# Expert stream of a two-block network: the copy of gathered rows traced ahead of the second split, the split of the middle columns traced one block later

## The chip, the cores and the metric

The kernel runs on one NeuronCore of a Trainium2 chip. The metric is the device time of one execution in microseconds; the time given for a kernel is the median of its runs. Engines are named as in the profile: PE is the tensor engine, PEld its weight loads, DVE the vector engine, ACT the scalar engine, POOL GpSimd, and SP the engine that issues the loads of weights.

## What is computed

The program is two blocks of two layers each. The first block is a sparse attention mixed with a gated delta rule. Each layer of the second block has a mixer, a mixture of experts and a gated addition. The change lies in the mixture of experts, which is run twice. Of 512 tokens, each goes to 2 of 32 experts:

```python
def expert_block(args):
    idx, e = args
    xb = x_pad[idx]
    hb = jax.nn.silu(xb @ w_gate[e]) * (xb @ w_up[e])
    return hb @ w_down[e]
```

`w_gate` and `w_up` of an expert are 1024 x 512, `w_down` is 512 x 1024, all fp32: 6 MB of weights per expert. The time of the kernel is that of the whole program; the two expert stages are some 530 and 515 us of it.

## The kernel before

**Precision.** A product of fp32 operands is built from rounded parts. `split(h, l, x)` (L423) writes the rounded value `h` with an ACT copy (L425) and the rest `l = x - h` with a DVE subtraction (L426). PE then multiplies the rounded parts. For the last rows of a weight tile the product is instead done with the plain fp32 tile (`also`), and there the gathered rows are needed as one whole tile, `xf`.

**Experts in pairs.** `gather` (L1517) fetches the rows of two experts, 64 slots each, with one indirect DMA issued by POOL. After that PE transposes them in two halves into PSUM (tile `aux`, L1532), and each half is split into the tile `pk` (ACT copy L425, DVE subtraction L426). Of the second half ACT also copies the last 128 rows whole, into `xf` (L1538).

**Units.** `experts` (L1727) walks over units (e, k, part). For expert e, k = 0, 1 are the two 1 MB loads of `w_gate`, k = 2, 3 those of `w_up`, k = 4, 5 those of `w_down`; each load is used in two parts, except that of k = 5, which is one unit. The order is the eight units of gate and up of expert e, then the three of down of expert e - 1. The loop runs the splits of the weights `AHEAD` = 6 units in front of the matmuls: step n splits unit n (`cut`, ACT L425 and DVE L426, into `X` or `wh` and `wl`), then does the matmuls of unit n - 6 (`inner`, L1581 to L1584, or `outer`, L1609 to L1614). Loads go through 6 buffers `w`; SP issues a load (L1561) when the buffer's last user, PE or DVE, is done with it.

**What else stands at fixed steps.** When the sum of gate or of up is complete, ACT copies it from PSUM into `tmp` (L1765), which frees one of three `acc` buffers. In the second step of expert e, `middle` (L1586) makes the hidden columns of expert e - 1: PE folds (L1593), ACT takes the tanh (L1596), DVE multiplies twice (L1597, L1598) into `mth`, and `split` turns that into `hk` (ACT, then DVE). `hk` is used by `outer` at the end of expert e. In the step (2, 1) of every odd expert the second part of `gather` (transposes, `pk`, `xf`) for the next pair is traced. `finish` (ACT L1622, DVE L1623, POOL L1624) adds the two halves of the result and scatters it.

**Order.** `pin` (L1627) binds PE, DVE and ACT each to the order in which the steps are traced, so that an instruction which waits on one of these engines holds up everything traced behind it on this engine. Within one step the scheduler may reorder.

The matmul of a new expert's gate (L1581) takes the `acc` buffer of the up sum before it, so it waits for the second of the two `tmp` copies. In trace order ACT does that copy behind the splits of the unit six steps on.

Of the kernel before, what the change touches and what calls it, by code (L numbers as in the profile page):

```python
# [20 lines left out]
P = 128  # L21
# [14 lines left out]
BLK = 64  # L36
# [143 lines left out]
class Net:  # L180
# [1336 lines left out]
    def gather(self, table, idx, m):  # L1517

        nc = self.nc
        v, act, pe = nc.vector, nc.scalar, nc.tensor  # L1520
        xg = self.t([P, D], "xg", 2)
        nc.gpsimd.indirect_dma_start(out=xg[:m], out_offset=None, in_=table[:, :],  # L1522
                                     in_offset=bass.IndirectOffsetOnAxis(ap=idx, axis=0),
                                     bounds_check=S - 1, oob_is_err=False)
        yield
        n = m // BLK
        pk = self.t([P, KT, n, P], "pk", 2, FR)
        xf = self.t([P, n, BLK], "xf", 2)
        for half in range(2):
            tp = self.aux()  # L1530
            for k in range(4):
                pe.transpose(tp[:, k * m:(k + 1) * m], xg[:m, (4 * half + k) * P:(4 * half + k + 1) * P],  # L1532
                             self.ident[:m, :m])
            tv = tp[:, 0:4 * m].rearrange("p (k e t) -> p k e t", k=4, e=n)
            o = pk[:, 4 * half:4 * half + 4]
            self.split(o[:, :, :, 0:BLK], o[:, :, :, BLK:P], tv)
            if half:
                act.activation(xf, tv[:, 3], AF.Copy)  # L1538
        yield [(pk[:, :, e], xf[:, e]) for e in range(n)]

    def apart(self, ins, first):
# [7 lines left out]
    def weights(self, i, e, k, part=None):  # L1549

        src = self.a[("w_exp_gate_2", "w_exp_up_2", "w_exp_down_2")[k // 2]][i]
        n, first = (4, 0) if part is None else (2, 2 * part)
        w = self.t([P, n * S], *(("w", self.nw) if part is None else ("wo", 1)))
        first += k % 2 * 4
        if k < 4:
            at, ap = first * S, [[D * D_EXP // P, P], [1, n * S]]
        else:
            at, ap = first // 2 * P * D, [[D, P], [P * D, n // 2], [1, D]]  # L1560
        self.load = self.nc.sync.dma_start(w if k < 4 else w.rearrange("p (f n) -> p f n", n=D), bass.AP(  # L1561
            tensor=src.tensor, offset=src.offset + e * (D * D_EXP) + at, ap=ap))
        return w.rearrange("p (q n) -> p q n", n=S)
# [22 lines left out]
    def middle(self, gu):  # L1586

        nc = self.nc
        v, act, pe = nc.vector, nc.scalar, nc.tensor
        fp = self.aux()  # L1590
        for q in range(2):
            for f in range(4):
                pe.matmul(fp[:, (4 * q + f) * BLK:(4 * q + f + 1) * BLK], gu[q][:, f * P:(f + 1) * P], self.fold,  # L1593
                          start=True, stop=True)
        th = self.t([P, 4 * BLK], "mth", 2)
        act.activation(th, fp[:, 0:256], AF.Tanh, scale=0.5)  # L1596
        v.scalar_tensor_tensor(th, th, 1.0, fp[:, 0:256], op0=OP.add, op1=OP.mult)  # L1597
        v.scalar_tensor_tensor(th, th, 0.5, fp[:, 256:512], op0=OP.mult, op1=OP.mult)  # L1598
        hk = self.t([P, 4, P], "hk", 2, FR)
        hv = th.rearrange("p (f t) -> p f t", f=4)  # L1600
        self.split(hk[:, :, 0:BLK], hk[:, :, BLK:P], hv)
        return hk, hv

    def outer(self, pss, hid, k, h, l, also):

# [94 lines left out]
    def overflow(self, i, e, x, mp, ym):  # L1700

        room = lambda: self.t([P, S], "bc", 3)
        gu = []
        for up in range(2):
            ps = self.acc()
            for k in range(0, KT, 2):
                w = self.weights(i, e, 2 * up + k // 4, k // 2 % 2)
                m = 1 if k == KT - 2 else 2
                h, l = self.cut(w[:, 0:m])
                self.inner(ps, x, k, h[:, :m], l[:, :m], w[:, 1] if m == 1 else None)  # L1710
            gu.append(room())
            self.nc.scalar.activation(gu[up], ps, AF.Copy)
        hid = self.middle(gu)
        pss = [self.acc() for _ in range(2)]

        for k in (0, 1):
            self.outer(pss, hid, k, *self.cut(self.weights(i, e, 4, k)), None)
        w = self.weights(i, e, 5, 1)
        for c in range(2):
            self.nc.tensor.matmul(pss[c][0:BLK], hid[1][:, 3], w[:, c], start=False, stop=False, skip_group_check=True)  # L1720
        h, l = self.cut(self.weights(i, e, 5, 0))
        for c in range(2):
            for part in (h, l):
                self.nc.tensor.matmul(pss[c], hid[0][:, 2], part[:, c], start=False, stop=part is l)
        self.finish(pss, room, mp, ym)

    def experts(self, i, ws, xs2, pair, mp, ym, weights):  # L1727

        nc = self.nc
        act = nc.scalar
        units = []
        for e in range(N_EXP + 1):
            if e < N_EXP:
                units += [(e, k, part) for k in range(4) for part in range(2)]
            if e:
                units += [(e - 1, 4, 0), (e - 1, 4, 1), (e - 1, 5, 0)]
        ready = deque()
        acc, gu, hid, g = {}, {}, {}, None  # L1740
        self.pinned = [None, None, {}]
        for n in range(len(units) + AHEAD):
            if n < len(units):
                e, k, part = units[n]
                if part == 0 and (e, k) not in ws:
                    ws[e, k] = self.weights(i, e, k)
                w = ws[e, k]
                m = 1 if k in (1, 3) and part else 2
                also = w[:, 3] if m == 1 else w[:, 2:4] if k == 5 else None
                h, l = self.cut(w[:, 2 * part:2 * part + m], n // 4 % 2)  # L1750
                ready.append((h[:, :m], l[:, :m], also))
            self.pin()
            if n < AHEAD:
                continue
            e, k, part = units[n - AHEAD]
            if k < 4:
                if (k, part) == (0, 0) and e % 2 == 0 and e + 2 < N_EXP:
                    g = pair(e // 2 + 1)
                    next(g)
                if (k % 2, part) == (0, 0):  # L1760
                    acc[e] = self.acc()
                self.inner(acc[e], xs2[e // 2][e % 2], 4 * (k % 2) + 2 * part, *ready.popleft())
                if (k % 2, part) == (1, 1):
                    gu.setdefault(e, []).append(self.tmp())
                    act.activation(gu[e][-1], acc[e], AF.Copy)  # L1765
                if (k, part) == (0, 1) and e:
                    hid[e - 1] = self.middle(gu.pop(e - 1))
                if (k, part) == (2, 1) and e % 2 and e + 1 < N_EXP:
                    xs2.append(next(g))
                if (e, k, part) == (2, 2, 0):  # L1770
                    wt = weights()
            else:
                r = k % 2 * 2 + part
                if e == N_EXP - 1 and r == 0:
                    hid[e] = self.middle(gu.pop(e))
                if r == 0:
                    acc[e, "y"] = [self.acc() for _ in range(2)]
                self.outer(acc[e, "y"], hid[e], r, *ready.popleft())
                if r == 2:
                    self.apart(self.finish(acc.pop((e, "y")), self.tmp, mp[:, e:e + 1], ym), e)  # L1780
            self.pin()
        return wt
# [175 lines left out]
```

## Time and profile before

| | |
|---|---|
| median of 3 runs | 3080.62 us (3080.24 to 3084.62) |
| profiled execution, its own time | 3084.05 us |
| its span | 3082.3 us |
| busy share of the span | PE 93%, PEld 70%, DVE 80%, ACT 57%, POOL 15% |
| expert stages in the span | about 1584 to 2116 us and 2460 to 2974 us |

The span is that of the profiled instructions, and the execution's own time has 1.75 us more around it. In a row of instructions "L426 DVE TENSOR_TENSOR X<-w,X" names line, engine, operation, output and inputs; "x2" says that two equal ones were merged; the value in brackets is the engine's idle time before, and whose end released it. A pair, below, is the time of two experts, from one gathered pair to the next.

### The profile page before, as it was taken

The page shows a single profiled execution, that of the slowest core. Times are in us where ns is not written, and L with a number is a line of the kernel's source. Part 1 is how long each engine was busy: PE and PEld are TensorE (multiplying, and loading weights), DVE is VectorE, ACT ScalarE, POOL GpSimd, SP SyncE. Part 2 cuts the span into 40 slices and gives each one's busy share as a digit, 9 for nine tenths or more (in the row PEclk, how much of TensorE's full clock was granted, in tenths as well). Part 3 has the DMA queues.
Part 4 walks back from the last instruction along what each step waited for, and adds up shares of the span by engine and source line. Part 5 has one row for each costly group of instructions (what it writes and reads, how often), then busy time and mean ns, then how long its engine had stood idle before and what let it go on. Part 6 is the DMA issues. An engine that isn't in the chain of part 4 may idle for free.

```text
span 3082.3 us, 39081 instructions
## 1 busy us (share of the span) xinstructions
PE 2881.6 (93%) x13517; PEld 2160.2 (70%) x13517; DVE 2464.3 (80%) x4540; ACT 1756.1 (57%) x2953; POOL 472.8 (15%) x457
## 2 busy tenths in 40 slices
PE   7998999999999999999979999998998799999987
PEld 6677778886787778878856666665776566666656
DVE  7899787867999578855558888887789588888876
ACT  3454343544454433542357877776476577777874
POOL 1111110011121010120011121111122111121112
PEclk9999999999999999999989999999999899999998
DMA  5211122242222222241259999997123399999981
GB/s 156 82 62 62 62 77 69 83 128 94 74 62 61 77 69 79 86 130 62 95 216 396 406 404 401 407 399 277 65 86 110 151 385 405 404 408 408 406 313 59
DMA packets 248663, 599.29 MB, mean 194 GB/s; under 512 B 29212, under 2 KB 159726, under 8 KB 215694
## 3 DMA queue, kind: packets, MB, share of 16 engines
q1 hardware_dynamic: 237582, 567.38, 49.1%
q0 software_dynamic: 10880, 29.37, 2.7%
q8 instruction: 108, 1.77, 0.2%
q14 instruction: 93, 0.76, 0.1%
HBM read 573.60 MB, written 31.49 MB: 196 GB/s over the span
## 4 chain that ended last, share of the span: by engine, by line
PE 38%; issue 33%; DVE 18%; POOL 7%; ACT 3%; DMA 2%; POOLq 0%; SPq 0%; ACTq 0%; DVEq 0%
PE acc L522 9%; PE acc L521 9%; PE acc L520 9%; POOL ym L1624 4%; DVE wl L426 3%; DVE tmp L953 2%; PE aux L432 1%; POOL xg L1522 1%; PE aux L463 1%; PE aux L843 1%; DMA xg<-xr,tk 1%; PE aux L1111 1%; PE aux L1106 1%; DVE r L1082 1%; DVE r L1081 1%
## 5 line engine op out<-in xcount | busy, mean ns | idle before, releaser
L425 ACT ACTIVATE wh<-w 128x1024 fp32r<-128x1024 f32 (+1 forms) x592 | 577.8, 1003 | 370.2 <-PE acc L521 323.0
L426 DVE TENSOR_TENSOR wl<-w,wh 128x1024 fp32r<-128x1024 f32 (+1 forms) x592 | 674.1, 1164 | 71.1 <-ACT wh L425 66.7
L520 PE MATMUL acc<-X,wh 128*128 128x512 f32 (+1 forms) x1504 | 606.3, 403 | 18.5 <-DVE tmp L898 6.4
L521 PE MATMUL acc<-X,wh 128*128 128x512 f32 (+1 forms) x1536 | 615.8, 401 | 0.6 <-DVE X L426 0.6
L522 PE MATMUL acc<-X,wl 128*128 128x512 f32 (+1 forms) x1504 | 601.9, 401 | 4.9 <-DVE wl L426 4.9
L426 DVE TENSOR_TENSOR X<-w,X 128x1024 fp32r<-128x1024 f32 (+1 forms) x352 | 380.9, 1122 | 64.0 <-ACT X L425 63.2
L425 ACT ACTIVATE X<-w 128x1024 fp32r<-128x1024 f32 (+1 forms) x352 | 326.7, 971 | 34.3 <-DMA w<-in_w_exp_gate_dram 10.1
L520 PEld LDWEIGHTS acc<-X,wh 128*128 128x128 f32 (+1 forms) x1504 | 285.3, 190 | 82.1 <-DVE tmp L898 7.3
L521 PEld LDWEIGHTS acc<-X,wh 128*128 128x128 f32 (+1 forms) x1536 | 291.3, 190 | 59.4 <-DVE X L426 1.2
L522 PEld LDWEIGHTS acc<-X,wl 128*128 128x128 f32 (+1 forms) x1504 | 284.8, 189 | 64.9 <-DVE wl L426 7.1
L1624 POOL DMA_INDIRECT ym<-yb,mp x64 | 136.0, 2125 | 811.9 <-DVE yb L1623 811.9
L1581 PE MATMUL acc<-X,pk 128*128 128x512 f32 x448 | 185.6, 414 | 18.2 <-ACT tmp L1765 12.6
L1581 PE MATMUL acc<-wh,pk 128*128 128x512 f32 x448 | 181.9, 406 | 15.5 <-ACT tmp L1765 15.5
L1584 PE MATMUL acc<-X,pk 128*128 128x512 f32 x448 | 185.9, 415 | 0.0
L1584 PE MATMUL acc<-wl,pk 128*128 128x512 f32 x448 | 183.5, 410 | 0.0
L1583 PE MATMUL acc<-w,xf 128*64 128x512 f32 x256 | 137.3, 618 | 0.0
L1584 PEld LDWEIGHTS acc<-X,pk 128*128 128x128 f32 x448 | 86.3, 193 | 66.0 <-DVE X L426 18.7
L1593 PEld LDWEIGHTS aux<-fold,tmp 128*128 128x128 f32 x1024 | 126.1, 194 | 8.8 <-ACT tmp L1765 3.5
L1584 PEld LDWEIGHTS acc<-wl,pk 128*128 128x128 f32 x448 | 84.5, 189 | 65.8 <-issue 16.2
L479 POOL TENSOR_TENSOR tmp<-tmp,tmp 128x512 f32<-128x512 f32 x60 | 86.4, 1444 | 280.9 <-ACT tmp L472 234.5
L1593 PE MATMUL aux<-fold,tmp 128*128 128x64 f32 x1024 | 123.2, 274 | 3.2 <-ACT tmp L1765 3.2
L1612 PE MATMUL acc<-w,mth 128*64 128x512 f32 x256 | 123.6, 605 | 0.0
(564 smaller groups left out, 5331.8 us busy)
## 6 DMA issues: line engine op xcount, KB each, us to landing
w<-in_w_exp_gate_dram SPq DMA_DIRECT2D x128, 1024.0 KB, 8.0
w<-in_w_exp_up_dram SPq DMA_DIRECT2D x128, 1024.0 KB, 7.8
w<-in_w_exp_down_dram SPq DMA_DIRECT2D x128, 1024.0 KB, 8.4
w<-in_w_in_dram SPq DMA_DIRECT2D x72, 1024.0 KB, 5.1
w<-in_w_in_a_dram SPq DMA_DIRECT2D x12, 1024.0 KB, 5.0
w<-in_w_out_dram SPq DMA_DIRECT2D x8, 1024.0 KB, 5.0
w<-in_w_ple_gate_dram SPq DMA_DIRECT2D x8, 1024.0 KB, 12.1
X<-ym SPq DMA_DIRECT2D x16, 512.0 KB, 5.4
```

The lines of the kernel that those rows point to most:

```text
L425: self.nc.scalar.activation(h, x, AF.Copy)
L426: self.nc.vector.tensor_sub(l, x, h.bitcast(F32))
L479: nc.gpsimd.tensor_add(t, tot[0], sq)
L520: mm(ps, wh[:, k], xh[k], start=(k == 0), stop=False)
L521: mm(ps, wh[:, k], xl[k], start=False, stop=False)
L522: mm(ps, wl[:, k], xh[k], start=False, stop=(k == kt - 1))
L1581: pe.matmul(ps, pk[:, k + q], h[:, q], start=(k + q == 0), stop=False)
L1583: pe.matmul(ps[0:BLK], xf, also, start=False, stop=False, skip_group_check=True)
L1584: pe.matmul(ps, pk[:, k + q], l[:, q], start=False, stop=also is not None)
L1593: pe.matmul(fp[:, (4 * q + f) * BLK:(4 * q + f + 1) * BLK], gu[q][:, f * P:(f + 1) * P], self.fold, start=True, stop=True)
L1612: pe.matmul(pss[c][0:BLK], hv[:, 3], also[:, c], start=False, stop=False, skip_group_check=True)
L1624: return nc.gpsimd.indirect_dma_start(out=ym[:, :], out_offset=bass.IndirectOffsetOnAxis(ap=mp, axis=0), in_=y, in_offset=None, bounds_che ...
```

## The change

In `gather` the copy to `xf` is traced ahead of the second half's split. `middle` becomes a generator: it stops in front of the split of `hk`, and `experts` resumes it one block later, in the step (1, 0) in place of (0, 1). For the last expert and for the overflow path the two parts stay together.

```diff
             o = pk[:, 4 * half:4 * half + 4]
-            self.split(o[:, :, :, 0:BLK], o[:, :, :, BLK:P], tv)
             if half:
                 act.activation(xf, tv[:, 3], AF.Copy)
+            self.split(o[:, :, :, 0:BLK], o[:, :, :, BLK:P], tv)
...
         v.scalar_tensor_tensor(th, th, 0.5, fp[:, 256:512], op0=OP.mult, op1=OP.mult)
+        yield
         hk = self.t([P, 4, P], "hk", 2, FR)
         hv = th.rearrange("p (f t) -> p f t", f=4)
         self.split(hk[:, :, 0:BLK], hk[:, :, BLK:P], hv)
-        return hk, hv
+        yield hk, hv
...
-        hid = self.middle(gu)
+        hid = list(self.middle(gu))[1]
...
                 if (k, part) == (0, 1) and e:
-                    hid[e - 1] = self.middle(gu.pop(e - 1))
+                    mid = self.middle(gu.pop(e - 1))
+                    next(mid)
+                if (k, part) == (1, 0) and e:
+                    hid[e - 1] = next(mid)
...
                 if e == N_EXP - 1 and r == 0:
-                    hid[e] = self.middle(gu.pop(e))
+                    hid[e] = list(self.middle(gu.pop(e)))[1]
```

The order on PE, POOL and SP is the same before and after; only ACT and DVE differ. On ACT, from the split of `hk` for one expert to the `tmp` copy at the next pair's start (first stage, experts 3 and 4), the order before is:

```order
L425 ACTIVATE hk_15180<-mth_15176 128x4x64
L425 ACTIVATE wh_15185<-w_15183 128x1024
L425 ACTIVATE wh_15193<-w_15183 128x1024
L1765 ACTIVATE tmp_15200<-acc_15154 128x512
L425 ACTIVATE X_15204<-w_15202 128x1024
L425 ACTIVATE X_15214<-w_15212 128x1024
L425 ACTIVATE pk_15221<-aux_15223 128x8x64
L425 ACTIVATE pk_15221<-aux_15230 128x8x64
L1538 ACTIVATE xf_15222<-aux_15230 128x128
L425 ACTIVATE X_15238<-w_15212 128x1024
L425 ACTIVATE X_15247<-w_15245 128x1024
L1765 ACTIVATE tmp_15253<-acc_15207 128x512
```

With the change the same place on ACT reads:

```order
L425 ACTIVATE wh_15182<-w_15180 128x1024
L425 ACTIVATE hk_15190<-mth_15176 128x4x64
L425 ACTIVATE wh_15193<-w_15180 128x1024
L1766 ACTIVATE tmp_15200<-acc_15154 128x512
L425 ACTIVATE X_15204<-w_15202 128x1024
L425 ACTIVATE X_15214<-w_15212 128x1024
L425 ACTIVATE pk_15221<-aux_15223 128x8x64
L1537 ACTIVATE xf_15222<-aux_15230 128x128
L425 ACTIVATE pk_15221<-aux_15230 128x8x64
L425 ACTIVATE X_15238<-w_15212 128x1024
L425 ACTIVATE X_15247<-w_15245 128x1024
L1766 ACTIVATE tmp_15253<-acc_15207 128x512
```

One split of a weight tile now stands ahead of the copy into `hk`, and `xf` stands ahead of the second copy into `pk`. On DVE, at the same expert's middle columns, the order before is:

```order
L1597 SCALAR_TENSOR_TENSOR mth_15176<-mth_15176,aux_15167 128x256
L1598 SCALAR_TENSOR_TENSOR mth_15176<-mth_15176,aux_15167 128x256
L426 TENSOR_TENSOR hk_15180<-mth_15176,hk_15180 128x4x64
L426 TENSOR_TENSOR wl_15186<-w_15183,wh_15185 128x1024
L426 TENSOR_TENSOR wl_15194<-w_15183,wh_15193 128x1024
```

With the change:

```order
L1597 SCALAR_TENSOR_TENSOR mth_15176<-mth_15176,aux_15167 128x256
L1598 SCALAR_TENSOR_TENSOR mth_15176<-mth_15176,aux_15167 128x256
L426 TENSOR_TENSOR wl_15183<-w_15180,wh_15182 128x1024
L426 TENSOR_TENSOR hk_15190<-mth_15176,hk_15190 128x4x64
L426 TENSOR_TENSOR wl_15194<-w_15180,wh_15193 128x1024
```

One subtraction of a weight tile now stands between the second multiplication of `mth` and the subtraction into `hk`. DVE's two subtractions into `pk` keep their place.

## Rows read from the trace of the kernel before

**Rows 1.** The page, 40 slices of the span: PE's and the DMA engines' busy tenths.

```profile
PE   7998999999999999999979999998998799999987
DMA  5211122242222222241259999997123399999981
```

**Rows 2.** Table by stretch: stretch, length, busy us per engine (count), PEclk, DMA share, GB/s.

```profile
1655.00:2085.00 430.00, 418.04 (x1768) 267.60 (x1768) 381.32 (x443) 341.11 (x483) 73.39 (x37) 1.00 1.00 403
2548.00:2943.00 395.00, 385.46 (x1632) 247.13 (x1632) 351.53 (x409) 314.31 (x446) 66.30 (x34) 1.00 1.01 406
1600.00:1632.00 32.00, 30.70 (x132) 19.85 (x131) 26.30 (x31) 23.36 (x33) 3.76 (x2) 1.00 1.02 424
1753.93:1786.57 32.64, 32.10 (x136) 20.60 (x136) 29.24 (x35) 26.19 (x38) 5.63 (x3) 1.00 1.01 414
1786.57:1820.12 33.55, 32.10 (x136) 20.61 (x136) 29.34 (x35) 26.18 (x38) 6.49 (x3) 1.00 1.01 403
```

**Rows 3.** Waits, 1655 to 2085 us: who waited for whom, us in total, times, longest.

```profile
ACT hk L425 <- DVE mth L1598: 59.5, 26, 2.6
ACT xf L1538 <- DVE pk L426: 22.0, 13, 1.7
PE acc L1581 <- ACT tmp L1765: 12.1, 14, 1.5
```

**Rows 4.** Groups of PE, stages 1584:2116 and 2460:2974: busy, mean ns | idle before, releaser.

```profile
L1581 PE MATMUL acc<-X,pk 128*128 128x512 f32 x224 | 92.8, 414 | 9.7 <-ACT tmp L1765 7.0 <-DVE pk L426 2.7
L1581 PE MATMUL acc<-wh,pk 128*128 128x512 f32 x224 | 90.8, 405 | 8.3 <-ACT tmp L1765 8.3
...
L1581 PE MATMUL acc<-wh,pk 128*128 128x512 f32 x217 | 88.3, 407 | 7.2 <-ACT tmp L1765 7.2
L1581 PE MATMUL acc<-X,pk 128*128 128x512 f32 x215 | 88.0, 409 | 5.6 <-ACT tmp L1765 5.6
```

**Rows 5.** Timeline at a pair's end, 1817 to 1821 us: start, length, engine, [idle <-releaser].

```profile
1817.61 0.28 ACT L1538 ACTIVATE xf<-aux 128x128 f32<-128x128 f32 x1 [1.71 <-DVE pk L426]
1817.79 1.99 ACT L425 ACTIVATE X<-w 128x1024 fp32r<-128x1024 f32 x2
1819.68 0.59 ACT L1765 ACTIVATE tmp<-acc 128x512 f32<-128x512 f32 x1
...
1818.87 2.36 DVE L426 TENSOR_TENSOR X<-w,X 128x1024 fp32r<-128x1024 f32 x2 [1.29 <-ACT X L425]
...
1820.32 0.50 PE L1581 MATMUL acc<-wh,pk 128*128 128x512 f32 x1 [1.45 <-ACT tmp L1765]
```

**Rows 6.** Line L1561 in 1808.3 to 1808.45 us: one load, issue and time to landing.

```profile
L1561 SPq DMA_DIRECT2D w<-in_w_exp_gate_dram x1: 341/341/341, 1808.4 to 1808.4; - x1
...
DMA to landing us min/median/max: 7.6/7.6/7.6
```

**Rows 7.** Timeline around the middle columns, 1791 to 1795 us.

```profile
1791.73 0.38 ACT L1596 ACTIVATE mth<-aux 128x256 f32<-128x256 f32 x1
...
1793.87 0.42 DVE L1598 SCALAR_TENSOR_TENSOR mth<-mth,aux 128x256 f32<-128x256 f32 x1
...
1794.32 0.42 ACT L425 ACTIVATE hk<-mth 128x256 fp32r<-128x256 f32 x1 [2.21 <-DVE mth L1598]
```

**Rows 8.** Groups of ACT, weight splits, stretches 1655:2085 and 2548:2943: idle by releaser.

```profile
L425 ACT ACTIVATE wh<-w 128x1024 fp32r<-128x1024 f32 (+1 forms) x144 | 133.8, 971 | 2.4 <-DMA w<-in_w_exp_gate_dram 1.2 <-DMA w<-in_w_exp_up_dram 1.1
L425 ACT ACTIVATE X<-w 128x1024 fp32r<-128x1024 f32 (+1 forms) x143 | 132.7, 968 | 3.7 <-DMA w<-in_w_exp_gate_dram 1.9 <-DMA w<-in_w_exp_up_dram 1.6
...
L425 ACT ACTIVATE X<-w 128x1024 fp32r<-128x1024 f32 (+1 forms) x133 | 123.2, 968 | 2.9 <-DMA w<-in_w_exp_up_dram 2.3 <-DMA w<-in_w_exp_gate_dram 0.5
L425 ACT ACTIVATE wh<-w 128x1024 fp32r<-128x1024 f32 (+1 forms) x132 | 122.3, 971 | 1.4 <-DMA w<-in_w_exp_gate_dram 0.7 <-DMA w<-in_w_exp_up_dram 0.5
```

**Rows 9.** Second stage: a long wait of PE, and the stretch after it by engine.

```profile
2495.22 0.50 PE L1581 MATMUL acc<-wh,pk 128*128 128x512 f32 x1 [1.99 <-ACT tmp L1765]
...
2496.50:2503.30 6.80, 6.80 (x25) 5.60 (x23) 6.37 (x9) 4.37 (x9) 2.24 (x1) 0.51 1.01 394
```

## The prediction

> **What bounds the kernel now.** I read the page first. In its slices PE is at 9 tenths almost throughout, and the DMA engines reach 9 only in two stretches [rows 1]. These are the two expert stages, the only places the change touches, so the rest of the program counts as unchanged.
>
> Then the table by stretch, for the steady middle of both stages [rows 2]. In the first one, 13 pairs take 430 us, that is 33.08 us a pair. PE is busy for 418.04 us of it, 32.16 us a pair. DVE (381.32 us) and ACT (341.11 us) have far more room. The DMA share is 1.00. So three limits lie close together: PE's own work, the DMA engines, and whatever keeps PE waiting for the remaining 0.92 us a pair. The last two rows separate them: a pair of 32.64 us and one of 33.55 us have the same PE work, 32.10 us, in the same 136 matmuls [rows 2]. What differs is waiting.
>
> Next the waits [rows 3]. PE's waiting in that stretch is one entry: L1581, the first matmul of a gate, waits for ACT's `tmp` copy, 12.1 us in 14 waits. That is 0.93 us a pair, the whole difference between 33.08 and 32.16. ACT, on which PE waits, is itself held up by DVE at two places: the copy into `hk` (59.5 us in 26) and the copy to `xf` (22.0 us in 13). Both are instructions that the change moves.
>
> Last the timeline at one wait [rows 5]. ACT was free at 1815.90 (the start of `xf`, 1817.61, less its 1.71 us of waiting for DVE's subtraction into `pk`). Behind `xf` stand two splits of weights, 1.99 us, and then `tmp`, which ends at 1820.27. PE starts at 1820.32 and could have started 1.45 us earlier, at 1818.87. So the wait behind `xf` is passed on to PE through ACT's order, almost undiminished.
>
> **The change, part by part.** It adds and removes no instruction and no DMA. PE, POOL and SP keep their order, so no queue is passed.
>
> *`xf` ahead of the second split of `pk`.* `xf` now follows an ACT copy that waits for the same transposes, not for DVE. At the place of rows 5 it can run at about 1815.90, the splits behind it follow directly, and `tmp` comes 1.71 us earlier, ending near 1818.56. That is 0.3 us ahead of the 1818.87 at which PE is ready, so the wait of 1.45 us is gone. The second copy into `pk` comes later by `xf` itself, 0.28 us [rows 5]; `pk` is used by PE only after the new gate begins and after units already split, so I cost it at nothing. If that cover were missing, it would be 0.28 us in 30 places, 8 us. DVE also gains: it sat idle 1.29 us for the first split behind `xf` [rows 5].
>
> Is the load there in time when the split starts 1.71 us sooner? At the place of rows 5 the second of the two splits reads a load issued at 1808.4 that landed 7.6 us later, at 1816.0 [rows 6]; the split would now begin near 1817.1. Here there is 1.1 us to spare.
>
> *`hk` one block later.* ACT finished the tanh at 1792.11 and then waited 2.21 us for DVE's second multiplication [rows 7]. One split of a weight tile (1.99 us for two, so 1.0 us) now fills part of this; by itself 1.2 us of waiting are left, less if DVE runs earlier. The wait is put at 1.0 us shorter for each expert. Queued behind `hk` is only the next split, and PE needs `hk` in `outer`, six units later, so the delay of `hk` by one split is hidden by these units; without them it would be 1.0 us an expert. No PE wait starts at `hk` in rows 3, so I give this half no term of its own: it makes ACT and DVE earlier and so helps the first half hold. Its bounds are a loss of nothing and a gain inside the same 28.1 us below.
>
> *The sum.* All idle time before L1581 that ACT's `tmp` ended, in both stages whole, is 7.0 + 8.3 + 7.2 + 5.6 = 28.1 us [rows 4]. That is the upper bound of the direct gain. The 2.7 us on `pk` in the same group is the start of a stage and stays.
>
> What is late next is a load. ACT waits for loads today 1.2 + 1.1 + 1.9 + 1.6 = 5.8 us in 13 pairs and 2.3 + 0.5 + 0.7 + 0.5 = 4.0 us in 12 [rows 8], 0.39 us a pair or 12 us in some 31. With ACT earlier these waits grow, but they stand where ACT had been waiting for DVE anyway. I take half, 6 us, as what still reaches PE; the ends are 0 and all of 28.1 (rival A). The forecast is 28.1 - 6 = 22 us less. Against the profiled execution (3084.05 us) that is 3062; this execution is 3.4 us above the median, and from the median of 3080.62 us it gives **3059 us**.
>
> Can the DMA engines follow? A pair moves 403 GB/s x 430 us / 13 = 13.3 MB. In PE's 32.16 us that is 414 GB/s. The pair of 32.64 us ran at 414, and 32 us at the start of the first stage, while buffers were still filling, at 424 [rows 2], which would be 31.4 us a pair. So a share of 1.00 does not mean a fixed rate, and there is some 2% of room: enough, but no more.
>
> The Trainium skill (Perfetto Trace Analysis, Identifying the Most-Contended Engine) would have DMA judged by its throughput, because the occupancy of 16 engines misleads, and gives about 435 GB/s as a single core's ceiling. By it the 173 MB of the first stretch need an estimated 398 us, and the gain would be 28 us with no load in the way; no row here shows more than 424.
>
> **The rivals.**
>
> *A. The loads are the bound.* For it: the share of 1.00 and 1.01 in every stretch [rows 2]; an ACT that is earlier would only wait at the next split until its load lands, still in front of `tmp`, and PE would wait as now. Against it: the same share at 403, 414 and 424 GB/s, and only 9.8 us of ACT's waiting on loads in 25 pairs [rows 8]. If the mean stays at 403 to 406 GB/s the time stays at 3080; if half of the room is lost to it the gain is about 10 us, 3071. Chance 0.20, two in five of it a gain over 6 us.
>
> The Trainium skill (Perfetto Trace Analysis, What "DMA-bound" means) says that a kernel bound on its 16 DMA engines is helped by larger descriptors; by that rule a new order on ACT gives nothing, the time of this rival's first case. The trace agrees as far as the share goes, 1.00.
>
> *B. The change does not do what it says.* `xf` might wait for DVE in its new place too, or the wait might reappear at the `pk` copy or whole at `hk`. Against it: in the new order of ACT `xf` stands behind only a copy that DVE does not have to follow. Then 3078 to 3081. Chance 0.06.
>
> *C. Fewer but longer waits, and the clock.* A PE that has used up its short waits meets a late load in one piece. In the second stage PE waited 1.99 us, and from 2496.5 to 2503.3 its granted clock was 0.51, so 1.2 GHz in place of 2.4 [rows 9]. That cost (1 - 0.51) x 6.8 = 3.3 us on top, 5.3 us for such a wait. It decides from seven such waits on: 7 x 5.3 = 37 us outweigh the 28.1 us by over 6.2. Ten make 3080.6 - 28.1 + 53 = 3106 us. For it: the drop is there once. Against it: the granted clock is 1.00 in both steady stretches [rows 2], where the waits of PE were up to 1.5 us [rows 3], and the change shortens waits. Chance 0.08.
>
> **How the numbers follow.** The forecast has the remaining 0.66, and its own range is 3049 (all 28.1 us and the 3.3 us of the one clock drop) to 3068. A measurement of this kernel tells about 0.2%, 6.2 us, from no change. Faster: 0.66 + 0.4 x 0.20 = 0.74. Same: 0.6 x 0.20 + 0.06 = 0.18. Slower: 0.08. The range goes from 3048 to 3078, which takes in A where it leaves a gain, and leaves out C, most of B and A's case without gain, about 0.2.
>
> **What would show it.** Right: in the steady stretches a pair near 32.3 us, some 415 GB/s at the same share; PE's waits for `tmp` down from 28.1 us to 6 or so; no wait of ACT at `xf`; at `hk` about half of the 59.5 us or less; more waiting of ACT for loads. A is right if GB/s stays at 403 to 406 and ACT's waits for loads take over the 22 us of `xf`. C shows as a PEclk below 1.00 in the steady stretches. The forecast is wrong in its sum if PE's busy time in a pair is not 32.1 us any more, and wrong in its cause if PE's waits fall but those of `xf` do not.

## The result, and the profile after

The changed kernel takes **3049.58 us** (median of 5 runs, 3045.47 to 3053.86) against 3080.72 us beside it: ratio 0.989, interval 0.9877 to 0.9904. On a second chip it was 3048.83 us, ratio 0.9888 (0.9872 to 0.9905). Medians of before differ by up to 3.4 us from chip to chip, so experiments are compared below by ratios; a ratio of 0.9888 on the 3080.62 us shown at first is a gain of 34.5 us, one of 0.989 a gain of 33.9 us. The forecast was a gain of 22 us, 3059 us, with a range from 3048: the ratio 0.989 of 3080.62 us comes to 3046.7 us, just under it.

The gain lies in the two expert stages. From the start of the first fold (L1593) to the end of the last one, the first stage takes 496.5 us (1603.4 to 2099.9) where it took 514.7 (1603.4 to 2118.1), the second 496.5 (2442.6 to 2939.1) where it took 515.5 (2460.6 to 2976.1). That is 37.2 us; the span fell by 36.3, from 3082.3 to 3046.0. The two stages by stretch, before and then after (columns as in [rows 2]):

```profile
1603.40:2118.10 514.70, 498.38 (x2113) 318.98 (x2111) 455.40 (x538) 406.01 (x575) 85.00 (x43) 1.00 1.00 402
2460.60:2976.10 515.50, 500.54 (x2115) 321.81 (x2114) 456.14 (x540) 406.17 (x575) 82.76 (x43) 0.99 1.00 402
...
1603.40:2099.90 496.50, 494.04 (x2113) 319.93 (x2111) 454.00 (x539) 412.71 (x575) 82.00 (x43) 1.00 1.01 417
2442.60:2939.10 496.50, 494.07 (x2115) 319.93 (x2114) 454.39 (x539) 413.51 (x575) 84.49 (x43) 1.00 1.01 416
```

PE's busy time falls by 4.3 and 6.5 us, its idle time by 13.9 and 12.5 us. The page of after, PE and the DMA engines in 40 slices and what the DMA engines moved in each:

```profile
PE   8998999999999999999979999999998799999997
DMA  5221222233222222223239999998123299999981
GB/s 157 84 63 62 64 74 73 83 109 108 69 63 70 70 70 77 87 80 125 83 131 416 420 420 420 422 412 319 64 87 100 109 418 419 420 421 421 406 313 61
```

The tenths look as before [rows 1]; the rate is what moved. The table by stretch, after (columns as in [rows 2]: the steady middle of both stages, then two single pairs):

```profile
1655.00:2084.00 429.00, 429.00 (x1829) 277.65 (x1828) 392.46 (x457) 357.30 (x496) 72.53 (x38) 1.00 1.01 417
2476.00:2923.00 447.00, 446.17 (x1904) 288.65 (x1903) 409.30 (x477) 373.45 (x519) 78.20 (x40) 1.00 1.01 417
1654.57:1686.42 31.85, 31.85 (x138) 20.66 (x136) 29.14 (x35) 26.27 (x37) 5.50 (x3) 1.00 1.02 418
1782.14:1813.99 31.85, 31.85 (x137) 20.67 (x136) 29.78 (x36) 27.14 (x39) 6.17 (x3) 1.00 1.02 420
```

PE is busy in all 429.00 of 429.00 us. A pair takes 31.85 us where it took 33.08, and the loads come at 417 GB/s in place of 403, at a DMA share of 1.01 where it was 1.00. The waits of the same stretch, after (who waited for whom: us in total, times, longest):

```profile
ACT hk L425 <- DVE mth L1598: 23.4, 26, 1.5
...
ACT wh L425 <- DMA w<-in_w_exp_gate_dram: 13.4, 14, 2.6
ACT X L425 <- DMA w<-in_w_exp_gate_dram: 10.7, 13, 1.4
ACT wh L425 <- DMA w<-in_w_exp_up_dram: 7.7, 14, 1.3
ACT X L425 <- DMA w<-in_w_exp_up_dram: 7.6, 14, 1.0
ACT X L425 <- DMA w<-in_w_exp_down_dram: 3.0, 6, 0.9
ACT wh L425 <- DMA w<-in_w_exp_down_dram: 2.9, 6, 0.5
```

Against [rows 3]: ACT's 22.0 us at `xf` are gone, its 59.5 us at `hk` are 23.4, and its waits for loads grew from 5.8 us [rows 8] to 45.3 (the sum of the last six). PE's 12.1 us at `tmp` no longer appear. The groups of L1581, first stage and then second, after (busy, mean ns | idle before, releaser):

```profile
L1581 PE MATMUL acc<-X,pk 128*128 128x512 f32 x224 | 91.5, 409 | 2.7 <-DVE pk L426 2.7
L1581 PE MATMUL acc<-wh,pk 128*128 128x512 f32 x224 | 90.0, 402 | 1.3 <-ACT tmp L1766 1.3
...
L1581 PE MATMUL acc<-X,pk 128*128 128x512 f32 x217 | 87.4, 403 | 0.4 <-ACT tmp L1766 0.4
L1581 PE MATMUL acc<-wh,pk 128*128 128x512 f32 x217 | 87.3, 402 | 0.4 <-ACT tmp L1766 0.4
```

The 28.1 us of [rows 4] are 1.3 + 0.4 + 0.4 = 2.1 us. The timeline at a pair's end, after (start, length, engine, [idle before <-releaser]):

```profile
1775.19 0.58 ACT L425 ACTIVATE pk<-aux 128x512 fp32r<-128x512 f32 x1
...
1775.67 0.27 ACT L1537 ACTIVATE xf<-aux 128x128 f32<-128x128 f32 x1
1775.83 0.60 ACT L425 ACTIVATE pk<-aux 128x512 fp32r<-128x512 f32 x1
...
1776.30 2.08 ACT L425 ACTIVATE X<-w 128x1024 fp32r<-128x1024 f32 x2
...
1778.29 0.58 ACT L1766 ACTIVATE tmp<-acc 128x512 f32<-128x512 f32 x1
...
1780.30 0.40 PE L1581 MATMUL acc<-X,pk 128*128 128x512 f32 x1
1780.41 2.01 ACT L425 ACTIVATE wh<-w 128x1024 fp32r<-128x1024 f32 x2 [1.02 <-DMA w<-in_w_exp_up_dram]
```

The same place in a pair as in [rows 5]: `xf` has no bracket, `tmp` ends at 1778.87, and PE starts the new gate at 1780.30 without having waited. `tmp` now has 1.4 us to spare where it was 1.45 us late. The next bracket is a wait of ACT for a load, behind `tmp`.

### The profile page after: what moved, and what is told of

Read it like the earlier page. It is cut to its first block, busy times and chain, and to the rows that moved or that the text cites. A ratio compares the mean times of both kernels' runs of the same rounds, so it can differ in the third digit from the quotient of the medians.

```text
span 3046.0 us, 39081 instructions
## 1 busy us (share of the span) xinstructions
PE 2881.6 (95%) x13517; PEld 2167.3 (71%) x13517; DVE 2461.7 (81%) x4540; ACT 1769.5 (58%) x2953; POOL 470.6 (15%) x457
## 5 line engine op out<-in xcount | busy, mean ns | idle before, releaser
L425 ACT ACTIVATE wh<-w 128x1024 fp32r<-128x1024 f32 (+1 forms) x592 | 585.0, 1006 | 416.8 <-PE acc L521 325.4
L425 ACT ACTIVATE X<-w 128x1024 fp32r<-128x1024 f32 (+1 forms) x352 | 333.2, 976 | 76.6 <-DMA w<-in_w_exp_gate_dram 27.3
L1581 PE MATMUL acc<-X,pk 128*128 128x512 f32 x448 | 183.4, 409 | 6.0 <-DVE pk L426 5.6
L1584 PE MATMUL acc<-X,pk 128*128 128x512 f32 x448 | 185.3, 414 | 0.0
L1584 PE MATMUL acc<-wl,pk 128*128 128x512 f32 x448 | 182.9, 408 | 0.0
L1581 PE MATMUL acc<-wh,pk 128*128 128x512 f32 x448 | 180.0, 402 | 1.7 <-ACT tmp L1766 1.7
L1584 PEld LDWEIGHTS acc<-X,pk 128*128 128x128 f32 x448 | 85.9, 192 | 66.8 <-issue 17.9
L1584 PEld LDWEIGHTS acc<-wl,pk 128*128 128x128 f32 x448 | 84.2, 188 | 66.5 <-issue 17.9
L1593 PEld LDWEIGHTS aux<-fold,tmp 128*128 128x128 f32 x1024 | 124.3, 191 | 8.2 <-ACT tmp L1766 3.0
L1593 PE MATMUL aux<-fold,tmp 128*128 128x64 f32 x1024 | 121.6, 271 | 2.7 <-ACT tmp L1766 2.7
```

What stands on the lines that cost most here:

```text
L425: self.nc.scalar.activation(h, x, AF.Copy)
L1581: pe.matmul(ps, pk[:, k + q], h[:, q], start=(k + q == 0), stop=False)
L1584: pe.matmul(ps, pk[:, k + q], l[:, q], start=False, stop=also is not None)
```

## What the experiments had to tell apart

Three theories stood against each other for why the gain is larger than forecast, with the loads as a fourth. The letters are those of the expectations.

- **Pass-on (P)**, the prediction's own: what counts is `xf`'s wait, handed through ACT's order to the `tmp` copy behind it and so to PE. Then `xf` alone brings nearly all, `hk` alone nearly nothing.
- **Loop (L, later D)**: ACT and DVE wait for each other at `xf` and at `hk`, and DVE's chain sets the pair. Then either half alone brings the whole gain, and plain work added on ACT disappears in ACT's waits for loads.
- **ACT's time (W)**, put up after the first experiments: in before ACT had almost no time left. Busy 341.11 us [rows 2], 59.5 + 22.0 waiting for DVE [rows 3] and 5.8 for loads [rows 8] make 428.4 of 430 us. Without the loads that is 422.6 / 13 = 32.5 us a pair, more than the 31.85 us that PE needs. Then time taken from ACT counts at `hk` as at `xf`, until PE is the bound.

ACT's sum alone does not decide between the last two, since DVE's is as full. Its waits for ACT in the stretch of before, 1655 to 2085 us:

```profile
DVE X L426 <- ACT X L425: 17.6, 23, 1.3
DVE wl L426 <- ACT wh L425: 16.9, 25, 1.3
...
DVE hk L426 <- ACT hk L425: 12.6, 26, 0.5
```

With 381.32 us of work that is 428.4 of 430 us too. The change itself was run beside the first experiments, on their chip.

**The change again.**

> The change itself, on the same chip as the next three. Both theories: 31 us under before, near 3049 us, a pair of experts at 31.85 us with PE busy throughout. Theory P (pass-on): PE's waits for the tmp copy came from ACT's wait at xf alone, handed on through ACT's order, and the hk half gives next to nothing. Theory L (loop): ACT and DVE wait for each other at xf and at hk, and DVE's own chain, 29.34 us of work and 3.3 us of idle time, sets the pair of 32.65 us; whichever pieces of idle time go, PE's own 31.85 us bounds next.

It came to 0.9888, as told above.

**Each half alone.** `xf` ahead of the split, with `middle` in one piece as before; and the reverse, `middle` in two steps with `xf` behind the split:

```diff
+            if half:
+                act.activation(xf, tv[:, 3], AF.Copy)
             self.split(o[:, :, :, 0:BLK], o[:, :, :, BLK:P], tv)
-            if half:
-                act.activation(xf, tv[:, 3], AF.Copy)
```

> Only xf ahead of the second split; the split of hk where it was before. P: all of the gain, 3048 to 3053 us. L: DVE's chain loses the 1.29 us behind xf and keeps 2.0 us at hk, 31.4 us a pair, under PE's 31.85: also 3048 to 3053 us. Both: ACT's wait at hk stays near 2.2 us each, so this run tells the theories apart only together with the next one; 3065 or more would speak against both.

```diff
-                    hid[e - 1] = self.middle(gu.pop(e - 1))
+                    mid = self.middle(gu.pop(e - 1))
+                    next(mid)
+                if (k, part) == (1, 0) and e:
+                    hid[e - 1] = next(mid)
```

> Only the split of hk one block later; xf behind the second split as before. P: ACT still waits at xf, PE's waits for tmp stay above 20 us in total, 3072 to 3080 us. L: DVE's chain loses 2.0 us at hk and keeps 1.29 us behind xf, 30.6 us a pair, under PE's 31.85: PE's waits gone, 3048 to 3054 us, although ACT's waits at xf stay at 1.7 us each.

`xf` alone: 3057.53 us, ratio 0.9916 (0.9899 to 0.9933), a gain of 25.9 us. `hk` alone: 3062.59 us, ratio 0.9931 (0.9914 to 0.9948), a gain of 21.3 us. Each gain is good to some 5 us, and a difference between two of them to some 7. Their sum, 47, is more than the 34.5 of both. P and L both had 3048 to 3053 us for `xf` alone; for `hk` alone P had 3072 to 3080 and L 3048 to 3054. Neither run came in where either of them put it. The waits of `hk` alone, 1655 to 2084 us:

```profile
ACT hk L425 <- DVE mth L1598: 26.7, 26, 1.3
...
ACT xf L1538 <- DVE pk L426: 21.6, 13, 1.7
...
PE acc L1581 <- ACT tmp L1766: 3.1, 7, 0.9
```

This decides against pass-on as the whole account: the half that should give next to nothing gives 21.3 us. ACT's wait at `xf` is whole, 21.6 us of the 22.0, with the same longest wait of 1.7 us, and the `tmp` copy stands behind it as before; yet PE's waits for `tmp` fell from 12.1 to 3.1 us. So ACT must arrive earlier at `xf`, having lost less at `hk`. The waits of `xf` alone are the mirror image:

```profile
ACT hk L425 <- DVE mth L1598: 60.3, 27, 2.6
...
PE acc L1581 <- ACT tmp L1765: 1.3, 3, 0.6
```

ACT's budget in either, without loads: 349.73 + 60.3 = 410.0 and 353.75 + 26.7 + 21.6 = 402.1 of 429 us (busy times from the tables below), where before had 421.6 and after 380.7. At 13.3 pairs (413 GB/s x 429 us / 13.3 MB; 412 gives the same) that is 30.8 and 30.2 us a pair. Each half brings ACT's time below PE's 31.85, and the second half finds only the rest of the way to PE's bound. But by this average each half alone should have reached it, and a pair still takes 429 / 13.3 = 32.3 us: a margin of 1.0 or 1.7 us a pair is not enough, and why is not shown. Nor does a microsecond count the same everywhere: `xf` alone frees 22.0 us of ACT in the stretch and gains 25.9, `hk` alone frees 32.8 and gains 21.3. The tables by stretch, `xf` alone and `hk` alone:

```profile
1655.00:2084.00 429.00, 426.58 (x1812) 273.62 (x1811) 389.76 (x454) 349.73 (x493) 77.72 (x38) 1.00 1.01 413
```

```profile
1655.00:2084.00 429.00, 425.70 (x1812) 273.91 (x1811) 389.90 (x456) 353.75 (x495) 74.99 (x38) 1.00 1.01 412
```

**`xf` taken from ACT altogether.** Before, with the copy done by DVE, where nothing is waited for:

```diff
-                act.activation(xf, tv[:, 3], AF.Copy)
+                v.tensor_copy(xf, tv[:, 3])
```

> The kernel before, with xf copied by DVE in place of ACT, behind the second subtraction into pk; hk as before. ACT's wait at xf is gone without any new order of ACT's other work, and DVE has one copy of 128x128 more, some 0.3 us a pair. P: all of the gain, 3048 to 3053 us. L: DVE's chain is 29.34 + 0.3 + 2.0 = 31.6 us a pair, just under PE's 31.85: 3048 to 3057 us.

3055.39 us, ratio 0.9905 (0.9889 to 0.9922), a gain of 29.3 us, not told apart from `xf` alone (25.9). It lies in L's range, 3048 to 3057, and outside P's. ACT saves its wait and the copy's 0.28 us, DVE takes the work on.

**ACT's time given back, in doses.** The change, with 6, 12 or 3 copies on ACT of a small tile that nobody reads, behind the splits of `pk`:

```diff
             self.split(o[:, :, :, 0:BLK], o[:, :, :, BLK:P], tv)
+            if half:
+                for _ in range(6):
+                    act.activation(self.t([P, P], "idle", 1), self.ident, AF.Copy)
```

> The change, with 6 copies of 128x128 added on ACT right behind the second copy into pk, once a pair, some 1.1 to 1.7 us; they wait for nobody and nobody waits for them. Theory W: it is the time that ACT loses ahead of tmp that counts, whatever takes it; then this stands near e2_hk_only, which kept 1.7 us of waiting there: 3054 to 3064 us. Theory D: it was ACT and DVE waiting for each other; work of ACT alone takes the place of its waits for loads and of what is left at hk (some 70 us in 430 us of the changed kernel): 3047 to 3053 us.

> The same with 12 copies, some 2.2 to 3.4 us a pair, more than either wait of the kernel before. W: PE's waits for tmp are back, 3065 us or more. D: most is still taken out of ACT's waits for loads, 3049 to 3060 us.

> The change with 3 added copies on ACT (of 0.34 us each, as 6 took 2.04), 1.02 us a pair. Fit from the runs so far: the change has a free slack of some 0.85 us of ACT's time a pair, and each us of loss beyond it costs 15 to 18 us in all. Then 1.02 us cost 2 to 4 us over the change: 3050 to 3053 us. If there is no slack (cost from the first us): 15 us or more, 3063. If the slack is larger: no difference to the change.

| ACT's time added, us a pair | ratio (interval) | dearer than the change, us |
|---|---|---|
| 3 copies, 1.02 | 0.9892 (0.9876 to 0.9909) | 1 |
| 1.66, the wait at `xf` left in (`hk` alone, 21.6 / 13) | 0.9931 (0.9914 to 0.9948) | 13 |
| 6 copies, 2.04 | 0.9958 (0.9941 to 0.9974) | 22 |
| 12 copies, 4.08 | 1.0077 (1.006 to 1.0093) | 58 |

The last column is the difference of ratios to 0.9888, times 3080.62. It is good to some 7 us. Within that the first microsecond is free, and the second costs some 0.66 us in each of some 31 pairs ((22 - 1) / (1.02 x 31), good to 0.2). The row in the middle is no dose but `xf`'s wait for DVE, and it falls on the line of the doses: between 1 and 22 at 1.66 the line has 14. As far as these runs can tell, time that ACT waits for DVE costs what the same time of plain work costs. That speaks against D, which had 3047 to 3053 us for 6 copies (3067.69 measured) and 3049 to 3060 for 12 (3104.04). W had 3054 to 3064 and 3065 or more, so that its price for 6 copies was too low. All doses stand at one place, ahead of `tmp`; none was given at `hk`, and none to DVE. The timeline of the 6 copies, the same place in a pair as above, and the waits and the table of the stretch:

```profile
1813.42 0.28 ACT L1537 ACTIVATE xf<-aux 128x128 f32<-128x128 f32 x1
1813.58 0.61 ACT L425 ACTIVATE pk<-aux 128x512 fp32r<-128x512 f32 x1
1814.06 2.04 ACT L1541 ACTIVATE idle<-ident 128x128 f32<-128x128 f32 x6
```

```profile
ACT hk L425 <- DVE mth L1601: 31.1, 27, 1.3
...
PE acc L1584 <- ACT tmp L1769: 2.4, 6, 0.6
```

```profile
1655.00:2084.00 429.00, 426.50 (x1811) 273.76 (x1810) 389.05 (x454) 373.58 (x573) 75.91 (x38) 1.00 1.01 413
```

(The copies shift later lines by 3, so L1584 here is L1581.) PE's waits for `tmp` are back, with `xf` out of DVE's way and `hk` late. ACT's budget is (373.58 + 31.1) / 13.3 = 30.4 us a pair, near that of the two halves. The tables by stretch with 12 copies, and with 3, and the wait at `hk` with 3:

```profile
1655.00:2084.00 429.00, 413.55 (x1701) 266.50 (x1700) 369.47 (x429) 377.37 (x616) 72.29 (x36) 0.97 0.99 393
```

```profile
1655.00:2084.00 429.00, 429.00 (x1832) 278.32 (x1832) 394.85 (x459) 368.49 (x538) 72.12 (x38) 1.00 1.01 418
```

```profile
ACT hk L425 <- DVE mth L1601: 23.3, 27, 1.3
```

With 3, PE stays full, at ACT's 368.49 us of work in place of 357.30, a budget of (368.49 + 23.3) / 13.5 = 29.1 us a pair. So PE was full at 28.4 and 29.1 us a pair and no longer at 30.2. With 12, PE's granted clock is 0.97, 0.03 x 429 = 13 us in this stretch alone and some 20 us in both stages: it fell to 0.5 (1.2 GHz) behind long waits, such as one of 2.22 us for `tmp` at 1658.65 us. So its 58 us are not a price of ACT's time alone, and no price by the microsecond is read from them.

**The `tmp` copy moved, ACT's time left alone.** If only `tmp`'s place counted, running the splits 5 units ahead in place of 6 would help before, since `tmp` then stands one split earlier in ACT's order:

```diff
-AHEAD = 6
+AHEAD = 5
```

> The kernel before with splits 5 units ahead of the matmuls in place of 6: on ACT one split (1.0 us) less stands in front of each tmp copy, and the waits at xf and hk stay as they are (22 and 60 us in 430). If the place of tmp in ACT's order is what hands ACT's lost time on to PE: the free slack grows by about 1.0 us a pair, some 15 us less than before, 3060 to 3072 us. If the waits themselves set the pair (ACT's and DVE's chain): no gain, 3078 to 3084 us. If a lead of 5 is too short: slower.

> The change with splits 5 units ahead. PE's own work bounds already, so no gain: 3047 to 3052 us; over 3055 us if the lead of 6 is needed for the loads, which are then taken up later and issued later.

Before with 5 ahead: 3084.96 us, ratio 1.0011 (1.0001 to 1.0021), no gain. Its waits and its table, 1655 to 2084 us:

```profile
ACT hk L425 <- DVE mth L1598: 64.7, 26, 2.7
ACT xf L1538 <- DVE pk L426: 22.2, 13, 1.7
...
PE acc L1581 <- ACT tmp L1765: 1.3, 2, 0.7
```

```profile
1655.00:2084.00 429.00, 423.83 (x1768) 265.32 (x1768) 383.52 (x443) 339.48 (x482) 89.32 (x37) 1.00 1.01 404
```

PE's waits for `tmp` are all but gone, and the rate stays at 404 GB/s. What `tmp` no longer takes shows up as PE's busy time: its 1768 matmuls read 423.83 us where the same number read 418.04 [rows 2]. ACT's sum is 339.48 + 64.7 + 22.2 = 426.4 of 429 us, as full as before. `tmp` was only where the shortage showed. The change with 5 ahead gives 0.9897 (0.988 to 0.9913), not told apart from 6, so it is not a lead too short that hides a gain.

**What bounds it now.** Three more edits of the change. The first takes products away from PE and leaves ACT and the loads as they are; the kernel then leaves the last 128 rows of gate and up out of its sums:

```diff
-            if also is not None:
-                pe.matmul(ps[0:BLK], xf, also, start=False, stop=False, skip_group_check=True)
```

> The change without the plain fp32 products of gate and up (L1583 left out, so the last 128 rows of these weights are missing from the sums). PE's work falls from 31.85 to some 27.5 us a pair. If the loads bound next at the 424 GB/s seen in the first stage's start (31.4 us a pair): 14 us less, 3033 to 3038 us. If 418 is already all there is: 3047 to 3051 us. If loads have far more room: under 3000 us.

It took 3039.24 us, ratio 0.9866 (0.985 to 0.9883); 3033 to 3038 was put down for loads at 424 GB/s. The table by stretch, the time of a gate's load from issue to landing (median of the whole run), and PE's largest wait:

```profile
1655.00:2084.00 429.00, 386.56 (x1737) 268.87 (x1737) 394.88 (x462) 358.62 (x500) 78.61 (x38) 1.00 1.02 422
```

```profile
w<-in_w_exp_gate_dram SPq DMA_DIRECT2D x128, 1024.0 KB, 12.4
```

```profile
PE acc L1608 <- DVE hk L426: 17.7, 22, 1.2
```

PE has a tenth less to do and the time falls by only 0.0022, 7 us, with intervals that overlap. At 422 GB/s a pair's 13.3 MB take 31.5 us, right behind PE's 31.85, and a load lands 12.4 us after its issue where it took 9.1 with the change: issued earlier, it does not land earlier by as much. That points to the loads as the limit there. They are not shown to be the only one: PE also waits 17.7 us for `hk`, now late, and 24.5 us in front of the next gate, for `tmp` (16.6) and for DVE's result `yb` (7.9).

The second splits every odd expert's last part of up like the other parts, in place of multiplying it whole:

```diff
-            pe.matmul(ps, pk[:, k + q], l[:, q], start=False, stop=also is not None)
+            pe.matmul(ps, pk[:, k + q], l[:, q], start=False, stop=also is not None or k + q == KT - 1)
...
-                m = 1 if k in (1, 3) and part else 2
+                m = 1 if part and (k == 1 or k == 3 and e % 2 == 0) else 2
```

> The change, with the last 128 rows of up in odd experts split like the others in place of the plain fp32 product. PE saves some 0.7 us a pair, ACT and DVE get some 0.5 and 0.6 us more of 31.85 us, where they have 4.6 and 2.4. If the loads bound at 31.4 us a pair: 0.45 x 31 = 14 us less, 3034 to 3040 us. If the loads already bound: no change, 3047 to 3051. If DVE's chain bounds: 3050 or more.

3043.91 us, ratio 0.9885 (0.9868 to 0.9901), between what was put down for PE's work as the present bound (3034 to 3040) and for the loads (3047 to 3051): not told apart from the change's 0.9888, and no version here clearly beats the change. The third moves `hk` one more block:

```diff
-                if (k, part) == (1, 0) and e:
+                if (k, part) == (1, 1) and e:
```

> The change with the split of hk yet one block later. ACT's wait at hk, still some 51 us in both stages, falls to under 10 us. If PE's own work bounds the changed kernel (PE busy 429.00 of 429 us): no difference to the change, 3047 to 3051 us. If ACT's remaining waits still reach PE: 3 us or more less.

3052.52 us, ratio 0.9902 (0.9886 to 0.9919). ACT does not wait at `hk` any more. ACT's largest waits in the stretch:

```profile
ACT wh L425 <- DMA w<-in_w_exp_gate_dram: 25.7, 22, 2.5
...
ACT X L425 <- DMA w<-in_w_exp_gate_dram: 21.0, 19, 1.5
...
ACT wh L425 <- DMA w<-in_w_exp_up_dram: 9.7, 16, 1.3
```

The 23.4 us freed are spent waiting for loads, 71.7 us in all (six entries) after 45.3, and nothing is gained: ACT is no longer the bound.

## Why the prediction was right in direction and short in size

**Right.** The change costs no instruction, and `xf`'s wait goes to nothing. `hk`'s falls to 39% (23.4 of 59.5), for which half or less was asked; an expert's wait is 1.4 us shorter ((59.5 - 23.4) / 26) for 1.0 foretold. ACT's waits for loads grow, the rate is 417 GB/s for some 415 foretold, a pair 31.85 us for some 32.3. B fell with the first of these. A fell as the bound: the rate rose from 403 to 417, and ACT's 45.3 us for loads did not take the place of `xf`'s wait in front of PE. The rule of the Trainium skill (Perfetto Trace Analysis, What "DMA-bound" means), by which a new order on ACT would have given nothing, therefore did not apply: the share was 1.00, and the DMA engines were not the bound. C did not occur: the granted clock is 1.00 in both steady stretches.

**The step that failed: "so I give this half no term of its own".** The reason was that no PE wait starts at `hk`. True, and no evidence: `hk`'s waits and `xf`'s came out of the same time of ACT, and PE's wait showed only where ACT's shortage met PE. `hk` alone is worth 21.3 us; on top of `xf` it brings the 8.6 us by which 34.5 exceeds 25.9, good to some 7. The prediction's own sign of a wrong cause, PE's waits falling while those of `xf` do not, is what `hk` alone shows (12.1 to 3.1 us, and 22.0 to 21.6). Behind it stands an earlier reading, that DVE and ACT "have far more room". Busy 79% of the stretch, ACT had 1.6 us of 430 in which it neither worked nor waited for DVE or a load. The same sum for ACT, the one engine on which PE waits there, would have shown it from the rows of before, though not whether ACT or DVE sets the pace.

**A term that was too large: "I take half, 6 us, as what still reaches PE".** ACT's waits for loads became 45.3 us, eight times as many, and 2.1 us reach PE at `tmp`. ACT has room for them on average: 380.7 of 429 us without them, 28.4 us in each of 429 / 31.9 = 13.4 pairs. The 28.1 us as upper end of the direct gain were nearly reached.

**A term that was missing.** PE's work a pair was taken as 32.10 to 32.16 us. It is 31.85, which is the prediction's own sign of a wrong sum. Over both stages PE's busy time fell by 4.3 + 6.5 = 10.8 us; 3.3 us of that is the half clock of [rows 9], the other 7.5 us stood nowhere in the sum. With the 28.1 - 2.1 = 26.0 us of waiting that is 36.8 of the stages' 37.2 us. A PE that waits loses a little more than the wait shows: the first matmul after one is 0.50 us long [rows 5], a gate's first matmul without a wait 0.40 (timeline above). At one wait a pair that is some 3 us; where the rest of the 7.5 comes from is not shown.

Not settled: medians give a gain of 31 to 35 us and spans 36. The profiled execution of before was 3.4 us over its median and holds a stretch at half clock behind its long wait in the second stage [rows 9], 3.3 us by the prediction's working, that the profiled one of after does not have. Summed in slices of 3 us, the change's second trace loses 1.7 us to the clock in that stage, before with 5 ahead nothing. In how many runs it occurs was not tried. Open as well is whether ACT alone set the pace or ACT and DVE in turn, and why an average margin of 1.7 us a pair did not do.

## What to carry to other kernels

Add up, for every engine that the busiest one waits on, its busy time and its waits for third engines in the stretch; one that is busy 79% of the time can hold up the rest, and the wait entry on the busiest engine names only the place where it shows. Then waits taken from that engine count elsewhere too (here at `hk`, where nothing on PE waits), until the next bound; gains of several such edits are not added but cut off there. An instruction whose input comes late from another engine is cheapest traced behind work that is ready, and idle copies in rising doses tell how much slack is left, as long as PE's clock stays up.

## What the runs showed of the hardware

- A DMA share of 1.00 to 1.02 stood at 403 GB/s (before), 413 (`xf` alone), 417 (the change) and 422 (without the products): the share says nothing of the room left. The Trainium skill (Perfetto Trace Analysis, Identifying the Most-Contended Engine) judges DMA by its throughput and not by occupancy, and the runs agree. The most seen over such a stretch was 422 GB/s, under the some 435 that the same page of the Trainium skill gives for one core (Roofline).
- PE's short waits cost more than their length: a pair's PE work reads 32.10 us where it waited [rows 2] and 31.85 where it did not, in nearly the same number of matmuls (136 and 137 or 138). Part of it is the first matmul after a wait, 0.50 us for 0.40; the rest was not traced.
- PE's granted clock stayed at 1.00 (2.4 GHz) in the steady stretch of before, with waits of up to 1.5 us. It fell to 0.5 (1.2 GHz) behind a wait of 1.99 us in before [rows 9] and behind one of 2.22 us with 12 idle copies, whose stretch has 0.97.
